# Latent attention: the high and low parts of the values in one stationary, and a left-over column

## The chip, the cores and the metric

One Trainium2 core (trn2) runs the whole encoder layer in one launch. The metric is device microseconds of that core, the median of the runs. A core has five engines with a queue each: TensorE (PE; its weight loads are listed apart as PEld), VectorE (DVE), ScalarE (ACT), GpSimd (POOL) and SyncE (SP), which here only issues DMAs.

## The reference, cut to what matters

The layer has a Fourier mix, a latent attention (MLA), a cross-attention and a mixture of experts. The change is in the latent attention: 8 heads, 2048 queries and keys, 64 + 32 (rotary) dimensions for queries and keys, 64 for values.

```python
kv = (rms_norm(u_kv, g_kv_lat) @ w_kv_up).reshape(B, S, MLA_HEADS, QK_NOPE_DIM + V_HEAD_DIM)
k_nope, v = kv[..., :QK_NOPE_DIM], kv[..., QK_NOPE_DIM:]
...
s = (jnp.einsum("bqhd,bkhd->bhqk", qn_b, k_nope)
     + jnp.einsum("bqhd,bkd->bhqk", qr_b, k_rope))
p = jax.nn.softmax(s.astype(jnp.float32) * scale, axis=-1).astype(v.dtype)
return jnp.einsum("bhqk,bkhd->bqhd", p, v)
```

## The kernel before

All matmuls that matter are done in float32r (R in the code), which keeps fewer bits than float32. So each operand x is held as a high part (x rounded to R) and a low part (x minus the high part, again in R), and a product is three matmuls: high x high, high x low, low x high. `split` makes the two parts, ScalarE the high one by a copy, VectorE the low one by a subtraction; `mm3` does the three matmuls.

**The projection** (`phase_qkv`) makes queries, keys and values in 8 blocks of 256 tokens. `up_v` (L350) projects v for two tiles of 128 tokens, splits it into `vsh` (per head 64 columns and a 65th of ones) and `vsl` (64 columns), and writes both to HBM, `vh_s` and `vl_s`.

**The attention** (`phase_mla`, L850) works in 32 units, head h by chunk c of 512 queries, here named (h,c), and in each over 16 key tiles kt of 128 keys. For a key tile, `scores` (L882) does three matmuls into a PSUM tile `pst` of 128 keys x 512 queries; ScalarE takes the exponential of it twice, once rounded to R (`ph`, L893) and once in full (`pf`, L894); VectorE subtracts to give `pl` (L895). The maximum that keeps the exponential in range was put in as a 97th row of the queries beforehand: `max_steps` (L827) does, during a unit, 16 matmuls into `pmax` and as many VectorE reductions for the next unit, then transposes and copies the result (L845). `values` (L900) does three matmuls into `po`, 65 x 512: values high x ph, low x ph, high x pl. Row 64, from the ones, is the sum of the softmax. After the 16th key tile ScalarE copies `po` out (L911), and two DMAs write it to HBM; the division by the sum comes later, from `os_s`.

**What sets the order.** Nothing is scheduled by a planner; each engine's queue is in the order of the code. Key tile by key tile the loop at L940 does the scores of tile kt, one or two steps of the maximum for the next unit, the values of tile kt-2 (`pend`), and in 92 of 100 tiles one step of a background generator `bg` (`fourier`, L460). In its order, over the stage, the background makes Fourier weights (TensorE, ScalarE, VectorE), squares rows on ScalarE (L544), and four times scales a block x on VectorE (L561: eight products of x with a PSUM tile), folds it on GpSimd (L567 and L568, twice, 128x1024; then eight of 128x512, L583), splits the folds (L36, L37) and multiplies them. Pools set what can run ahead: `pst` has 2 PSUM banks, `po` 2, `pmax` 3, the background 1; `ph` and `pl` have 3 buffers in SBUF, `pf` 2. On GpSimd there is, beside the folds, one memset of a row of ones per head (L816).

The next head's keys and values are loaded by SP during units (h,0) and (h,1).

Of the kernel before, what the change touches and what calls it, by code (L numbers as in the profile page):

```python
# [10 lines left out]
F = mybir.dt.float32  # L11
R = mybir.dt.float32r
# [3 lines left out]
AF = mybir.ActivationFunctionType  # L16
OP = mybir.AluOpType
# [100 lines left out]
def phase_qkv(e):  # L118

    nc, tc = e.nc, e.tc  # L120
    with ExitStack() as ctx:
# [6 lines left out]
        wp = pool(ctx, tc, "wq", side="right")  # L128
# [3 lines left out]
        ps = pool(ctx, tc, "psq", 1, space=PSUM)  # L132
# [37 lines left out]
        vsh = wp.tile([P, H, 2, 65], R, name="vsh")  # L170
        vsl = wp.tile([P, H, 2, 64], R, name="vsl")
        nc.vector.memset(vsh[:, :, :, 64:65].bitcast(F), 1.0)
        xT = e.xT.rearrange("(k p) t -> p k t", p=P)
        XR, XB, SQ, LT, LN, LH = {}, {}, {}, {}, {}, {}

# [174 lines left out]
        def up_v(b):  # L350
            lh, ll = LH[b]
            for t in range(2):
                p = ps.tile([P, 512], F, name="pup", bufs=4)
                tt = slice(t * P, (t + 1) * P)
                for k in range(2):
                    mm3(nc, p, lh[3 + k][:, tt], ll[3 + k][:, tt], wvh[k], wvl[k], k == 0, k == 1)
                split(nc, vsh[:, :, t, 0:64], vsl[:, :, t], p.rearrange("p (h c) -> p h c", h=H))
            eng = nc.scalar if b + 1 == NB else nc.sync
            eng.dma_start(e.vh_s.rearrange("h p c -> p h c")[:, :, 130 * b:130 * b + 130],
                              vsh.rearrange("p h t c -> p h (t c)").bitcast(F))  # L360
            eng.dma_start(e.vl_s.rearrange("h p c -> p h c")[:, :, 128 * b:128 * b + 128],
                              vsl.rearrange("p h t c -> p h (t c)").bitcast(F))
# [12 lines left out]
        for k in range(8):  # L375
            w = wl1(k)
# [16 lines left out]
        for b in range(NB):  # L393
# [34 lines left out]
            elif b + 2 == NB:  # L428
                cs = slice(b * B, (b + 1) * B)
# [420 lines left out]
def phase_mla(e, keep):  # L850

    nc, tc = e.nc, e.tc
    scale = (ND + RD) ** -0.5
    with ExitStack() as ctx:
# [43 lines left out]
        OT = {}  # L898

        def values(h, c, kt, pr):  # L900
            ph, pl = pr
            if kt == 0:
                OT[h, c] = ps.tile([65, 512], F, name="po", bufs=2)
            o = OT[h, c]
            vh, vl = VT[h]
# [3 lines left out]
            if kt == 15:  # L909
                of = mp.tile([65, 512], F, name="of")  # L910
                nc.scalar.activation(of, OT.pop((h, c)), AF.Copy)  # L911
                cs = slice(c * 512, (c + 1) * 512)
                eng = nc.scalar if (h, c) == units[-1] else nc.sync
                eng.dma_start(e.os_s[h:h + 1, cs], of[64:65])
                eng.dma_start(e.o_s[h * 64:(h + 1) * 64, cs], of[0:64])
# [24 lines left out]
        for n, (h, c) in enumerate(units):  # L940
            if n + 3 < len(units):
                load_q(n + 3)
            for kt in range(16):
                if kt in (1, 9) and c < 2 and h + 1 < H:
                    (load_v if c else load_k)(h + 1, kt // 8)
                pend.append((h, c, kt, scores(h, c, kt)))
                for m, i in ahead.get(slot, ()):
                    if i == 0:
                        MX[m] = max_steps(e, QT[units[m]], KT[units[m][0]][0], mp,
                                          lambda shape: ps.tile(shape, F, name="pmax", bufs=3))  # L950
                    MX[m][i]()
                if len(pend) > 2:
                    values(*pend.pop(0))
                slot += 1
                if slot * RATE // 100 > (slot - 1) * RATE // 100:
                    next(bg, None)
                if (h and c == 0 or n == len(units) - 1) and kt in (4, 8, 12):
                    if kt == 4:
                        rs = recip(e, mp, nc.sync, h - 1) if c == 0 else recip(e, mp, nc.sync, h, 0, 1536)
                    next(rs)  # L960
        for u in pend:
            values(*u)
        for _ in bg:
            pass
    e.mx.close()
# [1061 lines left out]
```

## Time and profile before

| | |
|---|---|
| median of 3 runs | 3145.25 us (3144.8 to 3148.56) |
| the profiled execution | 3139.12 us, span 3137.3 us, mean granted clock 0.983 |
| TensorE busy over the span | 3013.9 us, 96% |
| VectorE, ScalarE, GpSimd busy | 1983.7, 1535.0, 485.5 us |
| latent attention | 280.6 to 1264.5 us of the span |

The profile lists instructions by engine, with the line of the kernel, the names of the tiles (out<-in) and their shapes; a line can be a helper's (L36, L37, L44 to L46). "Busy" is time in which an instruction of the engine is listed; matmuls are pipelined, so that one is listed for longer than the distance to the next. What an engine waited for stands in brackets. PEclk is the share of the full TensorE clock that was granted; 1.00 is the upper of its two levels, 2.4 GHz.

### The profile page before, as it was taken

What the parts mean: (1) busy time and instruction counts of PE and PEld (TensorE: products, weight loads), DVE (VectorE), ACT (ScalarE), POOL (GpSimd) and SP (SyncE); (2) the same over time, 40 slices, a digit from 0 to 9 for tenths busy, and PEclk for the clock granted to TensorE, in tenths of its full rate; (3) what the DMA queues carried; (4) which work ended last, traced back from release to release, by engine and by line L of the source; (5) the groups of instructions that cost most, each with busy time, mean ns of one, the idle gap of its engine ahead of it and who ended that gap; (6) DMA issues with size and microseconds to landing.
All of it is one profiled execution on the core that took longest, in us unless ns stands there. A gap on an engine that the chain in (4) does not pass through costs nothing.

```text
span 3137.3 us, 45989 instructions
## 1 busy us (share of the span) xinstructions
PE 3013.9 (96%) x18047; PEld 2560.7 (82%) x18047; DVE 1983.7 (63%) x3481; ACT 1535.0 (49%) x2491; POOL 485.5 (15%) x583
## 2 busy tenths in 40 slices
PE   7999999999999999999999996599999999999998
PEld 6997777677777667789788885599999999999998
DVE  5557878888877776665444445655555555555665
ACT  4444686666666666216433332244444444445554
POOL 1221003221200000101000002100010100003664
PEclk8999999999999999999999998799999999999999
DMA  5766152032121211465111113366767676667885
GB/s 194 216 209 187 47 175 73 22 80 63 28 71 44 71 35 46 145 199 203 57 41 68 55 61 110 130 199 197 221 209 216 212 223 204 209 202 238 302 304 203
DMA packets 322970, 452.46 MB, mean 144 GB/s; under 512 B 21329, under 2 KB 238801, under 8 KB 321410
## 3 DMA queue, kind: packets, MB, share of 16 engines
q1 hardware_dynamic: 290216, 373.08, 37.3%
q0 software_dynamic: 15216, 55.39, 5.8%
q10 hardware_dynamic: 17322, 21.06, 2.2%
q8 instruction: 142, 2.33, 0.3%
q14 instruction: 74, 0.61, 0.1%
HBM read 361.06 MB, written 88.28 MB: 143 GB/s over the span
## 4 chain that ended last, share of the span: by engine, by line
PE 89%; DVE 5%; ACT 2%; issue 2%; DMA 1%; POOL 0%; SPq 0%; POOLq 0%; ACTq 0%; DVEq 0%
PE pa L44 5%; PE pa L45 5%; PE pa L46 5%; PE pb L44 5%; PE pb L45 5%; PE pb L46 5%; PE pst L887 3%; PE pst L889 3%; PE pst L888 3%; PE po L908 3%; PE po L906 3%; PE pmax L835 3%; PE po L907 3%; PE co L44 2%; PE co L46 2%; PE co L45 2%
## 5 line engine op out<-in xcount | busy, mean ns | idle before, releaser
L1671 DVE TENSOR_TENSOR wl<-wr,wh 128x2048 fp32r<-128x2048 f32 x188 | 429.4, 2291 | 263.8 <-ACT wh L1670 263.8
L895 DVE TENSOR_TENSOR pl<-pf,ph 128x512 fp32r<-128x512 f32 x512 | 397.4, 776 | 204.8 <-ACT pf L894 200.2
L893 ACT ACTIVATE ph<-pst 128x512 fp32r<-128x512 f32 x512 | 306.9, 599 | 276.8 <-PE pst L889 273.7
L1670 ACT ACTIVATE wh<-wr 128x2048 fp32r<-128x2048 f32 x191 | 362.8, 1907 | 127.2 <-issue 53.7
L836 DVE TENSOR_REDUCE mt<-pmax 128x1 f32<-128x512 f32 x496 | 337.5, 681 | 0.0
L894 ACT ACTIVATE pf<-pst 128x512 f32<-128x512 f32 x512 | 305.3, 596 | 10.6 <-DVE pl L895 10.5
L44 PE MATMUL pa<-hh,wh 128*128 128x256 f32 x1024 | 292.5, 286 | 0.0
L45 PE MATMUL pa<-hl,wh 128*128 128x256 f32 x1024 | 290.1, 283 | 0.1
L46 PE MATMUL pa<-hh,wl 128*128 128x256 f32 x1024 | 289.8, 283 | 0.0
L45 PE MATMUL pb<-hl,wh 128*128 128x256 f32 x1024 | 289.8, 283 | 0.0
L44 PE MATMUL pb<-hh,wh 128*128 128x256 f32 x1024 | 289.8, 283 | 0.0
L46 PE MATMUL pb<-hh,wl 128*128 128x256 f32 x1024 | 289.7, 283 | 0.0
L908 PE MATMUL po<-pl,vh 128*65 128x512 f32 x512 | 203.0, 396 | 9.2 <-DVE pl L895 9.2
L887 PE MATMUL pst<-q,kl 96*128 96x512 f32 x512 | 206.8, 404 | 1.9 <-ACT pf L894 1.9
L889 PE MATMUL pst<-q,kh 97*128 97x512 f32 x512 | 203.2, 397 | 0.0
L888 PE MATMUL pst<-q,kh 96*128 96x512 f32 x512 | 202.2, 395 | 0.0
L906 PE MATMUL po<-ph,vh 128*65 128x512 f32 x512 | 202.0, 395 | 0.0
L907 PE MATMUL po<-ph,vl 128*64 128x512 f32 x512 | 201.1, 393 | 0.0
L835 PE MATMUL pmax<-kh,q 96*128 96x512 f32 x496 | 198.8, 402 | 1.9 <-DMA q<-qr_s 1.5
L45 PEld LDWEIGHTS pa<-hl,wh 128*128 128x128 f32 x1024 | 196.6, 192 | 1.0 <-DVE hl L37 0.4
L44 PEld LDWEIGHTS pa<-hh,wh 128*128 128x128 f32 x1024 | 196.5, 192 | 0.8 <-ACT hh L36 0.2
L46 PEld LDWEIGHTS pb<-hh,wl 128*128 128x128 f32 x1024 | 196.6, 192 | 0.0
(627 smaller groups left out, 7361.3 us busy)
## 6 DMA issues: line engine op xcount, KB each, us to landing
wr<-in_w_exp_gate SPq DMA_DIRECT2D x64, 1024.0 KB
wr<-in_w_exp_up SPq DMA_DIRECT2D x64, 1024.0 KB
wr<-in_w_exp_down SPq DMA_DIRECT2D x63, 1024.0 KB
xr<-in_xT SPq DMA_DIRECT2D x16, 512.0 KB
wr<-in_x SPq DMA_DIRECT2D x16, 512.0 KB
k_s<-put SPq DMA_DIRECT2D x16, 512.0 KB
q<-q_s SPq DMA_DIRECT2D x32, 256.0 KB
wt<-in_xf SPq DMA_DIRECT2D x32, 256.0 KB
```

The lines of the kernel that those rows point to most:

```text
L44: nc.tensor.matmul(ps, lh, rh, start=start, stop=False, **kw)
L45: nc.tensor.matmul(ps, lh, rl, start=False, stop=False, **kw)
L46: nc.tensor.matmul(ps, ll, rh, start=False, stop=stop, **kw)
L836: nc.vector.tensor_reduce(mt[:, t, j:j + 1], p, axis=AX.X, op=OP.max)
L887: nc.tensor.matmul(p, kl[:, ks], qh[0:96], start=True, stop=False)
L889: nc.tensor.matmul(p, kh[:, ks], qh, start=False, stop=True)
L893: nc.scalar.activation(ph, p, AF.Exp, scale=scale)
L894: nc.scalar.activation(pf, p, AF.Exp, scale=scale)
L895: nc.vector.tensor_sub(pl, pf, ph.bitcast(F))
L908: nc.tensor.matmul(o, vh[:, kt], pl, start=False, stop=kt == 15)
L1670: nc.scalar.activation(W[i][0], r, AF.Copy)
L1671: eng.tensor_sub(W[i][1], r, W[i][0].bitcast(F))
```

## The change

The values of a head are stored as one tile of 129 columns: 64 of the high parts, the ones, the low parts of columns 1 to 63, and as a 129th the low part of column 0. The first 128 are one stationary, and `po` becomes 128 x 512: rows 0 to 63 the high product, row 64 the sum, rows 65 to 127 the low product of columns 1 to 63. `values` does two matmuls with it, against `ph` and against `pl`. The 129th column times `ph` remains, to be added to row 0 of `po`. In six key tiles (`BY_PE`) a matmul with that one column does it. In the other ten, `scores` multiplies `ph` by the column (one number per key, a pointer to 128x1): in six of these on ScalarE, in four on GpSimd (`BY_POOL`); GpSimd adds the ten up in `acc`, and a matmul with ones sums `acc` over the partitions into row 0. This is the new `whole`, which runs before the scores of key tile 3 of the next unit. `whole` also merges the two halves: ScalarE copies rows 64 to 127 into `ol` and once more row 64, the sum, and VectorE adds rows 0 to 63, with `rest` (0 for partition 0, 1 elsewhere) keeping the sum out of row 0.

The second exponential is written over the scores in PSUM (`p`), `pf` goes, and VectorE subtracts from PSUM. `pst` gets 3 banks, `pmax` 2; `ph` 4 buffers, `pl` 2.

```diff
-                split(nc, vsh[:, :, t, 0:64], vsl[:, :, t], p.rearrange("p (h c) -> p h c", h=H))
+                p = p.rearrange("p (h c) -> p h c", h=H)
+                nc.scalar.activation(vs[:, :, t, 0:64], p, AF.Copy)
+                for c, to in ((slice(1, 64), slice(65, 128)), (slice(0, 1), slice(128, 129))):
+                    nc.vector.tensor_sub(vs[:, :, t, to], p[:, :, c], vs[:, :, t, c].bitcast(F))
...
-            p = ps.tile([P, 512], F, name="pst", bufs=2)
+            p = ps.tile([P, 512], F, name="pst", bufs=3)
...
-            ph = pp.tile([P, 512], R, name="ph")
-            pf = pp.tile([P, 512], F, name="pf", bufs=2)
-            pl = pp.tile([P, 512], R, name="pl")
+            ph = pp.tile([P, 512], R, name="ph", bufs=4)
+            pl = pp.tile([P, 512], R, name="pl", bufs=2)
             nc.scalar.activation(ph, p, AF.Exp, scale=scale)
-            nc.scalar.activation(pf, p, AF.Exp, scale=scale)
-            nc.vector.tensor_sub(pl, pf, ph.bitcast(F))
+            nc.scalar.activation(p, p, AF.Exp, scale=scale)
+            nc.vector.tensor_sub(pl, p, ph.bitcast(F))
+
+            if kt not in BY_PE:
+                w = VT[h][:, kt, 128:129].bitcast(F)
+                first = (h, c) not in AC
+                if first:
+                    AC[h, c] = mp.tile([P, 512], R, name="acc", bufs=1)
+                t = AC[h, c] if first else mp.tile([P, 512], F, name="part", bufs=2)
+                if kt in BY_POOL:
+                    nc.gpsimd.tensor_scalar(t, ph.bitcast(F), w, None, op0=OP.mult)
+                else:
+                    nc.scalar.activation(t, ph.bitcast(F), AF.Copy, scale=w)
+                if not first:
+                    nc.gpsimd.tensor_add(AC[h, c], AC[h, c].bitcast(F), t)
...
+        BY_PE, BY_POOL = (0, 1, 2, 7, 12, 15), (4, 6, 9, 11)
...
-            nc.tensor.matmul(o, vh[:, kt], ph, start=kt == 0, stop=False)
-            nc.tensor.matmul(o[0:64], vl[:, kt], ph, start=False, stop=False)
-            nc.tensor.matmul(o, vh[:, kt], pl, start=False, stop=kt == 15)
...
+            for i, t in enumerate(pr):
+                nc.tensor.matmul(OT[h, c], VT[h][:, kt, 0:128], t, start=kt == 0 and i == 0, stop=False, skip_group_check=True)
+            if kt in BY_PE:
+                nc.tensor.matmul(OT[h, c][0:1], VT[h][:, kt, 128:129], pr[0], start=False, stop=False, skip_group_check=True)
+
+        def whole(h, c):
+            o = OT.pop((h, c))
+            nc.tensor.matmul(o[0:1], e.ones[:, 0:1], AC.pop((h, c)), start=False, stop=True, skip_group_check=True)
+            ol = mp.tile([65, 512], F, name="ol", bufs=1)
+            of = ol[0:64]
+            nc.scalar.activation(of, o[64:128], AF.Copy)
+            nc.scalar.activation(ol[64:65], o[64:65], AF.Copy)
+            nc.vector.scalar_tensor_tensor(of, of, rest, o[0:64], op0=OP.mult, op1=OP.add)
...
+                if n and kt == 3:
+                    whole(*units[n - 1])
                 pend.append((h, c, kt, scores(h, c, kt)))
```

How this stands in the queues, first on TensorE before, for one key tile of unit (0,0), from the scores to the values of two tiles earlier:

```order
L887 MATMUL pst_3402<-q_152,kl_150 128x512
L888 MATMUL pst_3402<-q_152,kh_149 128x512
L889 MATMUL pst_3402<-q_152,kh_149 128x512
L835 MATMUL pmax_3412<-kh_149,q_3258 128x512
L906 MATMUL po_3322<-ph_3369,vh_3254 65x512
L907 MATMUL po_3322<-ph_3369,vl_3256 64x512
L908 MATMUL po_3322<-pl_3371,vh_3254 65x512
```

On TensorE with the change, key tile 2 of unit (0,1), the total of unit (0,0) behind it, and the first score of key tile 3:

```order
L887 MATMUL pst_3632<-q_3267,kl_150 128x512
L888 MATMUL pst_3632<-q_3267,kh_149 128x512
L889 MATMUL pst_3632<-q_3267,kh_149 128x512
L837 MATMUL pmax_3641<-kh_149,q_3271 128x512
L924 MATMUL po_3644<-ph_3599,va_3265 128x512
L924 MATMUL po_3644<-pl_3600,va_3265 128x512
L926 MATMUL po_3644<-ph_3599,va_3265 1x512
L930 MATMUL po_3327<-acc_3342,ones_76 1x512
L887 MATMUL pst_3655<-q_3267,kl_150 128x512
```

The three value matmuls have become two, with one of a single column (L926) in six of 16 tiles, and once a unit the matmul of the total (L930).

GpSimd in unit (2,2), before and with the change, where the background's folds d, x and f are made (L567, L568 and L583 have become L569, L570 and L585):

```order
L567 TENSOR_TENSOR d0_6675<-x_6150 128x1024
L568 TENSOR_TENSOR x_6150<-x_6150 128x8x128
L567 TENSOR_TENSOR d1_6710<-x_6150 128x1024
L568 TENSOR_TENSOR x_6150<-x_6150 128x8x128
L583 TENSOR_TENSOR f_6748<-x_6150 128x512
```

```order
L907 TENSOR_TENSOR acc_6645<-acc_6645,part_6733 128x512
L569 TENSOR_TENSOR d0_6741<-x_6210 128x1024
L570 TENSOR_TENSOR x_6210<-x_6210 128x8x128
L903 TENSOR_SCALAR part_6753<-ph_6748,va_4895 128x512
L907 TENSOR_TENSOR acc_6645<-acc_6645,part_6753 128x512
L907 TENSOR_TENSOR acc_6645<-acc_6645,part_6771 128x512
L569 TENSOR_TENSOR d1_6779<-x_6210 128x1024
L570 TENSOR_TENSOR x_6210<-x_6210 128x8x128
L903 TENSOR_SCALAR part_6791<-ph_6786,va_4895 128x512
L907 TENSOR_TENSOR acc_6645<-acc_6645,part_6791 128x512
L585 TENSOR_TENSOR f_6816<-x_6210 128x512
```

Additions of the tiles 8, 9, 10 and 11, and two multiplications, now stand between the folds.

ScalarE with the change, in the same unit, from the exponentials of key tile 13 to those of key tile 15:

```order
L892 ACTIVATE ph_6824<-pst_6820 128x512
L893 ACTIVATE pst_6820<-pst_6820 128x512
L905 ACTIVATE part_6829<-ph_6824,va_4895 128x512
L892 ACTIVATE ph_6841<-pst_6837 128x512
L893 ACTIVATE pst_6837<-pst_6837 128x512
L905 ACTIVATE part_6846<-ph_6841,va_4895 128x512
L847 ACTIVATE q_5853<-pmax_6849 1x512
L37 ACTIVATE fh_6861<-f_6816 128x512
L892 ACTIVATE ph_6869<-pst_6865 128x512
```

Before, only exponentials, L845 (now L847) and the split of f stood there; the scaled copies (L905) of tiles 13 and 14 are new, and each needs one of the two `part` buffers.

## Rows read from the trace of the kernel before

**Rows 1.** Busy time by stretch: the stage, then units (1,0), (1,1), (1,3), (2,2), (3,1), (4,1), (7,3).

```profile
core 0: us, PE busy (x) PEld busy (x) DVE busy (x) ACT busy (x) POOL busy (x), PEclk, DMA share, GB/s
280.60:1264.50 983.90, 966.59 (x4417) 697.89 (x4416) 772.60 (x1224) 660.12 (x1295) 119.77 (x93) 1.00 0.24 66
396.30:424.00 27.70, 26.73 (x117) 18.95 (x116) 20.80 (x34) 25.75 (x64) 1.15 (x1) 1.00 0.90 255
424.00:451.10 27.10, 26.77 (x117) 18.98 (x116) 20.65 (x33) 26.10 (x65) 0.00 (x0) 1.00 0.70 226
478.10:511.40 33.30, 30.49 (x142) 21.67 (x141) 31.47 (x41) 20.18 (x38) 18.93 (x14) 1.00 0.06 16
577.00:608.20 31.20, 27.75 (x118) 18.77 (x118) 30.76 (x42) 19.52 (x36) 14.40 (x6) 1.00 0.07 18
673.10:703.30 30.20, 27.55 (x121) 19.25 (x120) 28.36 (x40) 18.60 (x35) 11.97 (x5) 1.00 0.17 53
...
795.60:829.60 34.00, 31.34 (x147) 22.36 (x146) 30.91 (x42) 20.67 (x40) 14.82 (x8) 1.00 0.17 47
1240.40:1264.50 24.10, 24.04 (x103) 16.35 (x102) 11.90 (x18) 18.33 (x35) 0.00 (x0) 1.00 0.11 29
```

**Rows 2.** Timeline of TensorE over one key tile: start in us, duration in us, instruction.

```profile
703.35 0.39 PE L887 MATMUL pst<-q,kl 96*128 96x512 f32 x1
...
704.27 0.39 PE L906 MATMUL po<-ph,vh 128*65 128x512 f32 x1
704.50 0.40 PE L907 MATMUL po<-ph,vl 128*64 128x512 f32 x1
704.74 0.39 PE L908 MATMUL po<-pl,vh 128*65 128x512 f32 x1
704.97 0.40 PE L887 MATMUL pst<-q,kl 96*128 96x512 f32 x1
```

**Rows 3.** Timeline of ScalarE in unit (1,0), one key tile with a square.

```profile
411.84 0.64 ACT L544 ACTIVATE wt<-wt 128x512 f32<-128x512 f32 x1
412.36 0.21 ACT L544 ACTIVATION_READ_ACCUMULATOR wt<-wt 128x1 f32 x1
412.45 0.61 ACT L893 ACTIVATE ph<-pst 128x512 fp32r<-128x512 f32 x1
412.93 0.62 ACT L894 ACTIVATE pf<-pst 128x512 f32<-128x512 f32 x1
413.41 0.66 ACT L544 ACTIVATE wt<-wt 128x512 f32<-128x512 f32 x1
```

**Rows 4.** Timeline of VectorE and GpSimd in unit (2,2), beside the first folds.

```profile
589.44 0.68 DVE L895 TENSOR_TENSOR pl<-pf,ph 128x512 fp32r<-128x512 f32 x1
589.59 2.79 POOL L567 TENSOR_TENSOR d<-x 128x1024 f32<-128x1024 f32 x1 [55.24 <-DVE x L561]
590.04 0.68 DVE L836 TENSOR_REDUCE mt<-pmax 128x1 f32<-128x512 f32 x1
590.64 0.67 DVE L561 TENSOR_TENSOR x<-x,bg 128x512 f32<-128x512 f32 x1
591.24 1.70 DVE L895 TENSOR_TENSOR pl<-pf,ph 128x512 fp32r<-128x512 f32 x1
```

**Rows 5.** Timeline of ScalarE in the projection: a copy with a pointer as scale, one without.

```profile
55.09 0.71 ACT L39 ACTIVATE wkh<-wr,gk 128x512 fp32r<-128x512 f32 x1
55.70 0.61 ACT L36 ACTIVATE xh<-xr 128x512 fp32r<-128x512 f32 x1
56.23 1.04 ACT L205 ACTIVATE wr<-wr 128x1024 f32<-128x1024 f32 x1
```

**Rows 6.** Groups on VectorE in the stage: count | busy us, mean ns | idle before.

```profile
L895 DVE TENSOR_TENSOR pl<-pf,ph 128x512 fp32r<-128x512 f32 x512 | 397.4, 776 | 204.8 <-ACT pf L894 200.2 <-PE pst L888 1.1 <-PE po L907 0.8
...
L561 DVE TENSOR_TENSOR x<-x,bg 128x512 f32<-128x512 f32 x32 | 21.6, 674 | 0.0
```

**Rows 7.** Groups on GpSimd over the whole span.

```profile
L583 POOL TENSOR_TENSOR f<-x 128x512 f32<-128x512 f32 x16 | 24.7, 1548 | 36.3 <-DVE fl L37 35.9
L567 POOL TENSOR_TENSOR d<-x 128x1024 f32<-128x1024 f32 x8 | 22.3, 2790 | 135.9 <-DVE x L561 135.9
L568 POOL TENSOR_TENSOR x<-x 128x1024 f32<-128x1024 f32 x8 | 21.7, 2718 | 0.6
...
L583 POOL TENSOR_TENSOR f<-d,d 128x512 f32<-128x512 f32 x16 | 20.6, 1287 | 97.9 <-DVE fl L37 97.9
...
L1338 POOL TENSOR_SCALAR h<-x,cy 128x1024 f32<-128x1024 f32 x2 | 2.3, 1128 | 404.4 <-ACT hTh L36 396.9 <-DVE cy L63 7.5
```

**Rows 8.** Busy time in a stretch of the projection, columns as in rows 1.

```profile
150.00:280.00 130.00, 125.21 (x966) 121.06 (x965) 76.37 (x169) 50.81 (x95) 33.30 (x41) 0.97 0.66 204
```

More of the change, by code (lines that the diff above doesn't have):

```diff
@@ L23 @@
 FW, QL, KVL, RD, ND, VD = 512, 384, 256, 32, 64, 64
+VW = 129
 class Env:
@@ L169, in phase_qkv @@
         ssx = wp.tile([P, 16], F, name="ssx")
-        vsh = wp.tile([P, H, 2, 65], R, name="vsh")
-        vsl = wp.tile([P, H, 2, 64], R, name="vsl")
-        nc.vector.memset(vsh[:, :, :, 64:65].bitcast(F), 1.0)
+        vs = wp.tile([P, H, 2, VW], R, name="vs")
+        nc.vector.memset(vs[:, :, :, 64:65].bitcast(F), 1.0)
         xT = e.xT.rearrange("(k p) t -> p k t", p=P)
@@ L356, in up_v @@
                     mm3(nc, p, lh[3 + k][:, tt], ll[3 + k][:, tt], wvh[k], wvl[k], k == 0, k == 1)
-                split(nc, vsh[:, :, t, 0:64], vsl[:, :, t], p.rearrange("p (h c) -> p h c", h=H))
+                p = p.rearrange("p (h c) -> p h c", h=H)
+                nc.scalar.activation(vs[:, :, t, 0:64], p, AF.Copy)
+                for c, to in ((slice(1, 64), slice(65, 128)), (slice(0, 1), slice(128, 129))):
+                    nc.vector.tensor_sub(vs[:, :, t, to], p[:, :, c], vs[:, :, t, c].bitcast(F))
             eng = nc.scalar if b + 1 == NB else nc.sync
[L359 to L362, printed above, removed]
+            eng.dma_start(e.va_s.rearrange("h p c -> p h c")[:, :, 2 * VW * b:2 * VW * (b + 1)],
+                          vs.rearrange("p h t c -> p h (t c)").bitcast(F))
         e.K0 = mla_keys(e, e.m0)
@@ L869, in load_k, with load_v @@
             nc.sync.dma_start(t[64:96].bitcast(F), e.kr_s[:, i])
-        def load_v(h, i, a=0, b=16):
-            n = 65 - i
+        def load_v(h, a, b):
             if a == 0:
-                VT.setdefault(h, []).append(vp.tile([P, 16, n], R, name="vh" if i == 0 else "vl"))
-            t, src = VT[h][i], (e.vh_s, e.vl_s)[i]
-            nc.sync.dma_start(t[:, a:b].rearrange("p t c -> p (t c)").bitcast(F), src[h][:, a * n:b * n])
+                VT[h] = vp.tile([P, 16, VW], R, name="va")
+            nc.sync.dma_start(VT[h][:, a:b].rearrange("p t c -> p (t c)").bitcast(F), e.va_s[h][:, a * VW:b * VW])
         def load_q(n):
@@ L900, in values @@
+            return ph, pl
+        OT, AC = {}, {}
+        BY_PE, BY_POOL = (0, 1, 2, 7, 12, 15), (4, 6, 9, 11)
+        rest = mp.tile([64, 1], F, name="rest", bufs=1)
+        nc.gpsimd.memset(rest, 1.0)
+        nc.gpsimd.memset(rest[0:1], 0.0)
         def values(h, c, kt, pr):
-            ph, pl = pr
             if kt == 0:
-                OT[h, c] = ps.tile([65, 512], F, name="po", bufs=2)
-            o = OT[h, c]
-            vh, vl = VT[h]
-            nc.tensor.matmul(o, vh[:, kt], ph, start=kt == 0, stop=False)
@@ L907, in values @@
-            nc.tensor.matmul(o[0:64], vl[:, kt], ph, start=False, stop=False)
-            nc.tensor.matmul(o, vh[:, kt], pl, start=False, stop=kt == 15)
[L909 to L915, printed above, removed]
+                OT[h, c] = ps.tile([P, 512], F, name="po", bufs=2)
@@ new lines, in values @@
+            for i, t in enumerate(pr):
[10 more added lines that the diff above has]
+            nc.vector.scalar_tensor_tensor(of, of, rest, o[0:64], op0=OP.mult, op1=OP.add)
+            cs = slice(c * 512, (c + 1) * 512)
+            eng = nc.scalar if (h, c) == units[-1] else nc.sync
+            eng.dma_start(e.os_s[h:h + 1, cs], ol[64:65])
+            eng.dma_start(e.o_s[h * 64:(h + 1) * 64, cs], of)
@@ L925, in phase_mla @@
         bg = e.bg
-        for i in range(2):
-            load_v(0, i, 0, 14)
+        load_v(0, 0, 14)
         load_q(1)
         load_q(2)
-        for i in range(2):
-            load_v(0, i, 14, 16)
+        load_v(0, 14, 16)
         ahead, MX = {}, {}
@@ L944, in phase_mla @@
                 if kt in (1, 9) and c < 2 and h + 1 < H:
-                    (load_v if c else load_k)(h + 1, kt // 8)
+                    i = kt // 8
+                    if c:
+                        load_v(h + 1, 8 * i, 8 * i + 8)
+                    else:
+                        load_k(h + 1, i)
+                if n and kt == 3:
+                    whole(*units[n - 1])
                 pend.append((h, c, kt, scores(h, c, kt)))
@@ L949, in phase_mla @@
                         MX[m] = max_steps(e, QT[units[m]], KT[units[m][0]][0], mp,
-                                          lambda shape: ps.tile(shape, F, name="pmax", bufs=3))
+                                          lambda shape: ps.tile(shape, F, name="pmax", bufs=2))
                     MX[m][i]()
@@ L962, in phase_mla @@
             values(*u)
+        whole(*units[-1])
         for _ in bg:
@@ L1873, in run @@
 def run(e):
+    e.va_s = e.tc.dram_tile([H, P, 16 * VW], F, name="va_s")
     with ExitStack() as ctx:
```

1 line of the change is left out of this document (removed).

## The prediction

> **What bounds the kernel now.** I read the windows view first. The change lives in the latent attention, from 280.6 to 1264.5 us, and there TensorE is busy 966.6 of 983.9 us at the full granted clock; VectorE has 772.6, ScalarE 660.1, GpSimd 119.8 [rows 1]. So matmuls taken away count, as far as the engines that get the work can follow. Then the timeline of TensorE, because the durations printed for matmuls overlap: each of the seven matmuls of a key tile is listed with 0.39 to 0.40 us, yet they start 0.23 us apart, seven in 1.62 us [rows 2]. The price of a 512-column matmul is 0.232 us, not 0.395. The width of the stationary makes no difference to it (65 columns in the values, 128 in the scores).
>
> Next, where the stage is not TensorE's. In units (1,0) and (1,1) (396.3 to 451.1 us) ScalarE is busy 25.75 of 27.7 and 26.10 of 27.1 us [rows 1]: the Fourier background squares a row piece in each key tile, and ScalarE runs squares and exponentials without a gap, 1.57 us from one square to the next [rows 3]. And in units (1,3), (2,2), (3,1) and (4,1) TensorE lacks 2.81, 3.45, 2.65 and 2.66 us, 11.6 together [rows 1]: there GpSimd works through its folds, and the subtraction on VectorE with both inputs in SBUF takes 1.70 us beside a fold instead of 0.68, while the product that reads PSUM keeps its 0.67 [rows 4].
>
> **The change part by part.**
>
> *TensorE.* Before, 32 units x 16 tiles x 3 value matmuls = 1536. After, 32 x (16 x 2 + 6 + 1) = 1248. 288 fewer, x 0.232 = **-66.8 us**. The one-column matmul costs a whole 0.232: its 512 moving columns are the same.
>
> *ScalarE.* Added: six scaled copies a unit (192). The nearest row is a copy of 128x512 out of SBUF with a pointer as scale: 0.71 long, the next starts 0.61 later [rows 5]. 192 x 0.61 = 117 us. The output leaves in two copies instead of one, 32 x 0.48 = 15 us. Sum 660 + 132 = 792 of some 940 us: hidden on average, but not in (1,0) and (1,1). There 25.75 + 26.10 + 2 x (6 x 0.61 + 0.48) = 60.1 us, with 0.8 of waits that stay 61.0, where TensorE alone would come to 54.8 - 2 x 9 x 0.232 = 50.6: **+10.4 us** of the gain given back.
>
> *The second exponential in place.* No row shows ScalarE writing PSUM. From PSUM to SBUF it starts every 0.48 us [rows 3]. Below: a copy that reads SBUF takes 0.53 [rows 5], so the side of the memory moves 0.05, and I allow that as a gain, worth under 2 us since ScalarE bounds only two units. Above: reading and writing one bank in turn, twice 0.48. I take 0.48, the row nearest in form. The Trainium skill (ScalarE: Activation LUTs, Step-by-step: what each stage is for) says that ScalarE writes PSUM faster than SBUF, and gives no figure; no run here shows it, and by it the sum would lie toward that lower end.
>
> *VectorE.* The subtraction now reads one input from PSUM. Its mean was 776 ns; the product that also has one input in PSUM takes 674 and is not stretched beside GpSimd [rows 4, 6]. I take 0.67. The 32 new merges of two halves, 64x512, cost at most the same 0.67, 21 us. VectorE loses load on the whole. The Trainium skill (SBUF — State Buffer, Who interferes with whom) has the rule: two SBUF inputs contend with a GpSimd instruction that reads SBUF, one does not. The trace agrees (1.70 against 0.67). By it the subtraction is out of the contention for good; without it, at the stretched length beside a GpSimd that is now busy most of the time, VectorE would be the bound (last rival).
>
> *GpSimd.* Nine additions and four multiplications a unit. Addition 1.29 to 1.55 (a fold of this shape), multiplication half of 1.128 (128x1024) = 0.56 [rows 7]: I take 1.29, since the long value is from folds beside subtractions that will no longer contend. 32 x (11.6 + 2.3) = 443, with the 120 there is 563 of 940 us. The first addend comes at key tile 4, the total is needed before key tile 3 of the next unit, 15 tiles or 22 us later: 13.9 us of work fits, if nothing stands in between.
>
> In four units something does. In (2,2) GpSimd's order after the addition of tile 8 is fold, fold, multiply, add, add, fold, fold, multiply, add: 2 x (2.79 + 2.72) + 2 x 0.56 + 3 x 1.29 = 16.0 us [rows 7]. Tile 8's addition ends about 16 us into the unit (8 tiles x 1.55; 1.8 for 0.7 of scores, 0.48 and 0.6 of exponentials; 0.6; 1.3), so the last of these ends at 32. But "part" has two buffers: ScalarE's scaled copy of tile 14 has to wait for that addition, from 24 to 32, and behind it on ScalarE stand the split of the background's first fold f (ready 1.6 later) and the exponentials of tile 15. Those give TensorE its operand at 36 where it wants it at 27.3 (17.6 tiles x 1.55): 9 us lost. In (3,1) the same count gives f at 35.8, the operand of tile 18 at 38, wanted at 31: 7 us. In (1,3) and (4,1) the folds start between two units, ScalarE is held 2 to 3 us, and TensorE, which can run two tiles ahead, loses about 1.5 each. Together 19, in place of the 11.6 that go with the old contention: **+7.4 us**.
>
> *The rest.* pst gets three banks, pmax two, since PSUM now holds the exponential until the subtraction. pl goes from three to two buffers: the subtraction of tile k waits for the value matmuls of k-2, which stand just behind k's scores and end before k's second exponential does. Nothing. In the last unit ScalarE has 18.3 + 4.1 = 22.5 us where TensorE has 24.1 - 2.1 = 22.0; at the end the total, two copies and the merge stand before the last output DMA, 0 to 3 us; VectorE runs 3 x 0.60 a tile while it scales the background's x, now against tiles of 1.5: some 0.5 each time. **+4 us**. In the projection one more small VectorE instruction a token tile (16 x 0.68 at most, 11 us in 280) lies beside a TensorE that is busy 125.2 of 130 while VectorE has 76.4 [rows 8]; v goes out and comes back in half as many DMAs of the same bytes, so SP's queue only gets shorter. Nothing.
>
> Sum: -66.8 + 10.4 + 7.4 + 4 = **-45 us**. The profiled execution took 3139.1 us for a span of 3137.3, 6 us under the median of 3145.25; the difference goes onto the median: **3100 us**.
>
> **The rivals.**
> 1. *The folds cost little* (GpSimd gets to them later than I count, or the waits overlap): -66.8 + 10.4 - 11.6 + 1 = -67, 3078 us. For it: TensorE's lead, and that each fold's place can slip. Against: GpSimd's order is fixed. 0.14.
> 2. *GpSimd's chain is late in every unit.* At 1.55 to 1.69 an addition and 1.13 a multiplication [rows 7] it is 9 x 1.69 + 4 x 1.13 = 19.7 us plus 3.7 of background, over the 22 us: about 1 us lost a unit, 32 more, 3132 us. It decides from about 2.1 us per addition, or earlier where ScalarE is held by the two parts. 0.13.
> 3. *Slower: the exponential in place takes longer.* ScalarE has 792 us; at 0.96 instead of 0.48 it has 792 + 512 x 0.48 = 1038, and becomes the bound of a stage of 984: +54, 3199 us. From 0.28 us extra per exponential the gain shrinks, from 0.37 it is gone. For it: it reads and writes one bank. Against: nothing, but nothing shows it either. 0.09.
> 4. *The subtraction still collides with GpSimd*: at 1.19 us, halfway from 0.68 to 1.70, VectorE has 772.6 - 397.4 + 512 x 1.19 + 21 = 1006 us [rows 1, 6] and is the bound: +22, 3167 us; it decides from 1.15. Against it stand 32 products at 0.67. 0.03.
>
> **How the numbers follow.** My forecast has 0.60, with 3085 to 3115 as its own range; 0.01 is left for the unforeseen. The range of 3076 to 3126 takes in most of the first rival and the better part of the second, and leaves out the slow cases. A measurement of this kernel tells about 0.2%, 6 us, from no change. Faster: the forecast, the first rival and three quarters of the second, 0.84. Slower: the last two, 0.12. Same: 0.04.
>
> **What would show it.** Right: value matmuls 0.23 apart and 288 fewer; units without background near 25 us; (1,0) and (1,1) longer than before, near 30, with ScalarE without a gap; the subtraction at 0.68 everywhere; waits of ScalarE on GpSimd additions and of TensorE in (2,2) and (3,1). Wrong: exponentials on the same PSUM tile spaced more than 0.55 us; additions over 1.6 us; TensorE waiting for the total at key tile 3 in ordinary units; units (2,2) and (3,1) shorter than 29 us.

## The result, and the profile after

The changed kernel takes 3186.99 us (median of 4 runs, 3185.13 to 3192.9) where the kernel before takes 3146.9: a ratio of 1.0131, interval 1.0113 to 1.0148. It is 40 us slower where 45 us less were forecast, and it lies outside the range.

The windows view of the changed kernel, over the stage and then the units (1,0), (1,1), (1,3), (2,2) and (7,3); columns as in [rows 1]:

```profile
279.50:1307.50 1028.00, 948.47 (x4125) 702.78 (x4123) 765.07 (x1256) 791.66 (x1516) 684.24 (x508) 0.98 0.24 64
402.90:433.70 30.80, 27.92 (x109) 19.83 (x108) 21.50 (x35) 30.66 (x72) 19.56 (x14) 0.94 0.86 240
433.70:464.70 31.00, 27.36 (x108) 18.26 (x107) 21.34 (x34) 30.87 (x73) 17.78 (x13) 1.00 0.62 188
493.90:527.60 33.70, 28.88 (x132) 21.81 (x131) 24.91 (x40) 23.95 (x47) 32.15 (x26) 1.00 0.12 30
596.70:634.20 37.50, 28.75 (x108) 19.73 (x107) 26.71 (x44) 23.35 (x42) 28.27 (x18) 0.85 0.09 25
...
1283.30:1307.70 24.40, 22.35 (x87) 15.30 (x87) 11.94 (x18) 21.25 (x40) 16.99 (x13) 1.00 0.12 28
```

Nearly the whole loss is in the stage: 1028.0 us instead of 983.9, 44 of the 47 us between the two spans (3184.5 and 3137.3). TensorE lacks 17 us of busy time there before [rows 1] and 80 now, so it has become an engine that waits, although no engine has taken its place as the bound: VectorE is busy for 765, ScalarE for 792, GpSimd for 684 us.

The groups of the changed kernel on the engines that took the work (GpSimd's over the span, the others in the stage: count | busy us, mean ns | idle before, and for what):

```profile
L907 POOL TENSOR_TENSOR acc<-acc,part 128x512 fp32r<-128x512 f32 x288 | 377.1, 1309 | 59.4 <-ACT part L905 40.5 <-ACT P4h L37 0.4
L903 POOL TENSOR_SCALAR part<-ph,va 128x512 f32<-128x512 f32 x128 | 205.0, 1601 | 256.9 <-ACT ph L892 142.0 <-PE po L924 74.2 <-PE pst L889 22.9
...
L894 DVE TENSOR_TENSOR pl<-pst,ph 128x512 fp32r<-128x512 f32 x511 | 352.0, 689 | 232.1 <-ACT pst L893 204.9 <-ACT part L905 12.1 <-issue 5.0
...
L893 ACT ACTIVATE pst<-pst 128x512 f32<-128x512 f32 x511 | 303.9, 595 | 0.0
L905 ACT ACTIVATE part<-ph,va 128x512 f32<-128x512 f32 x159 | 113.4, 713 | 23.6 <-POOL acc L907 23.4
```

The exponential in place, the subtraction, the addition and the scaled copy have the forecast prices. ScalarE's sum came out at 792 us, as forecast. The multiplication on GpSimd (L903) has not its price: 1.60 us where 0.56 was forecast.

What TensorE waits for stands in the waits of the changed kernel in the stage (engine, line, released by: us in total, times, longest):

```profile
PEld pmax L837 <- DVE mt L838: 93.9, 138, 2.9
...
PE pmax L837 <- DVE mt L838: 44.7, 63, 2.4
...
PE pmax L837 <- ACT q L847: 15.8, 8, 6.2
PE po L930 <- POOL acc L907: 4.2, 1, 4.2
```

A weight load's wait runs in part beside the matmul ahead of it, so the matmuls' own 44.7 us are nearer to what TensorE lost. Before, the matmul of the maximum waited for hardly anything; in the view of its tile, the waits ahead of `pmax` were these (us, times):

```profile
  DVE mn L839: 7.0, 7
  DVE mt L836: 2.3, 5
```

One such wait, from the timelines of ScalarE, TensorE and VectorE in the changed kernel (start in us, duration, engine, instruction, in brackets the wait), put in order of time, with the rows of other key tiles left out:

```profile
1139.75 0.50 PE L837 MATMUL pmax<-kh,q 96*128 96x512 f32 x1
...
1141.92 0.60 ACT L892 ACTIVATE ph<-pst 128x512 fp32r<-128x512 f32 x1 [0.17 <-POOL acc L907]
1142.41 0.59 ACT L893 ACTIVATE pst<-pst 128x512 f32<-128x512 f32 x1
1142.66 0.40 PE L889 MATMUL pst<-q,kh 97*128 97x512 f32 x1
1143.04 0.69 DVE L894 TENSOR_TENSOR pl<-pst,ph 128x512 fp32r<-128x512 f32 x1 [1.10 <-ACT pst L893]
1143.65 0.68 DVE L838 TENSOR_REDUCE mt<-pmax 128x1 f32<-128x512 f32 x1
1144.38 0.50 PE L837 MATMUL pmax<-kh,q 96*128 96x512 f32 x1 [1.32 <-DVE mt L838]
```

Read it from the end. The last matmul wants the bank that the first one filled, and that the reduction L838 has to empty. The reduction could have started at 1140.3, but on VectorE's queue it stands behind the subtraction of its key tile, and that waits for both exponentials of the tile. ScalarE was late with them here because two copies of the background had waited for VectorE (1.53 and 0.29 us). With three banks TensorE had one more key tile of time before it met this; with two, a ScalarE two tiles late stops it.

### The profile page after: what moved, and what is told of

It reads as the page before. It is cut to its first block, busy times and chain, and to the rows that moved or that the text cites. A ratio compares the mean times of both kernels' runs of the same rounds, so it can differ in the third digit from the quotient of the medians.

```text
span 3184.5 us, 46707 instructions
## 1 busy us (share of the span) xinstructions
PE 3000.1 (94%) x17759; PEld 2568.6 (81%) x17759; DVE 1979.5 (62%) x3529; ACT 1669.3 (52%) x2715; POOL 1049.7 (33%) x1001
## 4 chain that ended last, share of the span: by engine, by line
PE 55%; DVE 3%; issue 1%; POOL 1%; ACT 1%; DMA 0%; POOLq 0%; ACTq 0%; DVEq 0%
PE pa L45 5%; PE pa L46 5%; PE pa L47 5%; PE pb L45 5%; PE pb L46 5%; PE pb L47 5%; PE co L45 2%; PE co L47 2%; PE co L46 2%; PE sc L45 2%; PE sc L47 2%; PE sc L46 2%; PE py L45 2%; PE py L47 2%; PE py L46 2%
## 5 line engine op out<-in xcount | busy, mean ns | idle before, releaser
L894 DVE TENSOR_TENSOR pl<-pst,ph 128x512 fp32r<-128x512 f32 x512 | 352.7, 689 | 234.3 <-ACT pst L893 207.1
L907 POOL TENSOR_TENSOR acc<-acc,part 128x512 fp32r<-128x512 f32 x288 | 377.1, 1309 | 59.4 <-ACT part L905 40.5
L838 DVE TENSOR_REDUCE mt<-pmax 128x1 f32<-128x512 f32 x496 | 337.1, 680 | 0.0
L893 ACT ACTIVATE pst<-pst 128x512 f32<-128x512 f32 x512 | 304.5, 595 | 0.0
L1735 POOL DMA_INDIRECT x_s<-y,idx x24 | 62.9, 2620 | 731.6 <-ACT y L1870 637.6
L903 POOL TENSOR_SCALAR part<-ph,va 128x512 f32<-128x512 f32 x128 | 205.0, 1601 | 256.9 <-ACT ph L892 142.0
L837 PE MATMUL pmax<-kh,q 96*128 96x512 f32 x496 | 213.2, 430 | 63.5 <-DVE mt L838 44.7
L924 PE MATMUL po<-pl,va 128*128 128x512 f32 x512 | 205.7, 402 | 2.7 <-DVE pl L894 2.6
L924 PE MATMUL po<-ph,va 128*128 128x512 f32 x512 | 206.1, 403 | 1.2 <-ACT ph L892 1.2
L837 PEld LDWEIGHTS pmax<-kh,q 96*128 96x128 f32 x496 | 95.3, 192 | 134.3 <-DVE mt L838 93.9
```

The lines of the kernel that those rows point to most:

```text
L837: nc.tensor.matmul(p, qh[0:96, t * P:(t + 1) * P], kh[0:96, j * 512:(j + 1) * 512], start=True, stop=True)
L838: nc.vector.tensor_reduce(mt[:, t, j:j + 1], p, axis=AX.X, op=OP.max)
L893: nc.scalar.activation(p, p, AF.Exp, scale=scale)
L894: nc.vector.tensor_sub(pl, p, ph.bitcast(F))
L907: nc.gpsimd.tensor_add(AC[h, c], AC[h, c].bitcast(F), t)
L924: nc.tensor.matmul(OT[h, c], VT[h][:, kt, 0:128], t, start=kt == 0 and i == 0, stop=False, skip_group_check=True)
```

## The experiments

Each was timed beside runs of the kernel before on the same chip, whose median was between 3143.2 and 3144.6 us; ratios are to that.

**1. The bank alone**, in the kernel before:

```diff
-                                          lambda shape: ps.tile(shape, F, name="pmax", bufs=3))
+                                          lambda shape: ps.tile(shape, F, name="pmax", bufs=2))
```

> The kernel before with one edit: pmax has two PSUM banks instead of three. Theory A (the banks): the maximum matmul of tile k+2 waits for VectorE's reduction of tile k, which stands behind the subtraction of tile k, which waits for both exponentials; so already before any work is shared out, TensorE waits on pmax for 15 to 40 us and the time is 3160 to 3185. Theory B (the load: added copies on ScalarE, and GpSimd multiplications of 1.6 us, hold the units back): no difference beyond 6 us from 3147.

Measured: 3183.37 us, 1.0132 (1.0115 to 1.0149). This one number makes the kernel before as slow as the changed one. Its waits have the same pair (weight load, then matmul):

```profile
PEld pmax L835 <- DVE mt L836: 58.1, 81, 2.4
...
PE pmax L835 <- DVE mt L836: 31.6, 52, 2.2
```

**2. VectorE's reduction ahead of the subtraction**, in the changed kernel; both banks stay two:

```diff
-            nc.vector.tensor_sub(pl, p, ph.bitcast(F))
...
                     MX[m][i]()
+                ph, pl, p = pend[-1][3]
+                nc.vector.tensor_sub(pl, p, ph.bitcast(F))
```

> The changed kernel with one edit: VectorE's reduction of the maximum is issued ahead of the subtraction of the same tile, so that pmax comes free without waiting for the exponentials; same banks, same work on every engine. Theory A: TensorE's waits on pmax for a reduction, 45 us of its own and 94 of its weight loads in the changed kernel, fall below 20, and the time falls by 60 to 100 us, to 3085 to 3125. Theory B: the waits move to other instructions, and the time stays above 3165.

Measured: 3144.67 us, 0.9999 (0.9989 to 1.0009), 42 us under the changed kernel and between the two forecasts. Of the 42, about 9 are in unit (0,0), where the maximum of the next unit makes up to two steps a tile: 38.6 us in the changed kernel, 29.5 here. The matmul's wait for the reduction falls from 44.7 to 13.9 us. So the wait for the bank is about as large as the whole loss, but something else still eats the gain. Its waits in the stage show what is next:

```profile
ACT part L904 <- POOL acc L906: 30.8, 25, 5.9
...
PE pst L889 <- ACT q L847: 15.6, 9, 7.8
PE pmax L837 <- DVE mt L838: 13.9, 18, 1.4
```

**3. The bank given back to the maximum**, at the cost of the scores, order as in the change:

```diff
-            p = ps.tile([P, 512], F, name="pst", bufs=3)
+            p = ps.tile([P, 512], F, name="pst", bufs=2)
...
-                                          lambda shape: ps.tile(shape, F, name="pmax", bufs=2))
+                                          lambda shape: ps.tile(shape, F, name="pmax", bufs=3))
```

> The changed kernel with pmax at three banks and pst at two, as they were before; the exponential stays in place. Theory A: waits on pmax go, but now the scores of tile k+2 wait for the subtraction of tile k, which ends about as late as the reduction did: 3120 to 3175, with the wait now at the first score matmul. Theory B: above 3175, with TensorE waiting for units that ScalarE or GpSimd hold.

Measured: 3172.84 us, 1.0096 (1.0079 to 1.0113). The wait moves to the other tile:

```profile
PEld pst L887 <- DVE pl L894: 116.3, 212, 2.1
...
PE pst L887 <- DVE pl L894: 38.1, 65, 1.7
```

Now that the second exponential stays in PSUM until the subtraction, two banks are too few for the scores as well. Three of each was not tried: it takes one bank more than either kernel uses.

**4. The left-over column on TensorE in all 16 tiles**, nothing on ScalarE or GpSimd, order and banks as in the change:

```diff
-        BY_PE, BY_POOL = (0, 1, 2, 7, 12, 15), (4, 6, 9, 11)
+        BY_PE, BY_POOL = tuple(range(16)), ()
```

> The changed kernel with the left-over column done by TensorE in all 16 tiles: no scaled copies on ScalarE, nothing of it on GpSimd, and no total; TensorE has 1536 value matmuls as before. The banks stay at two for pmax. Theory A: TensorE's waits on pmax stay at 40 us or more over both its queues together, and the time is 3155 to 3190. Theory B: with the load gone the time is that of the kernel before or less, 3130 to 3150.

Measured: 3172.94 us, 1.009 (1.0067 to 1.0113). The kernel is slow without any shared work, 28 us over the kernel before with as many matmuls, so the sharing is not the cause of most of the loss.

**5. GpSimd's multiplication in another form**, in the kernel of experiment 2:

```diff
-                    nc.gpsimd.tensor_scalar(t, ph.bitcast(F), w, None, op0=OP.mult)
+                    nc.gpsimd.tensor_scalar(t, ph.bitcast(F), w, 1.0, op0=OP.mult, op1=OP.mult)
```

> The kernel with the reduction ahead of the subtraction, and GpSimd's four multiplications of a unit written with two operations (times w, times 1.0), the form that the kernel has on 128x1024 elements in 1.128 us. What is asked is the price. Theory C (the rest of the loss is GpSimd's chain: a multiplication of 1.59 us where 0.56 was forecast makes 18 us of GpSimd a unit, so that a scaled copy on ScalarE waits for its buffer, and behind it the 97th row and the exponentials): if the two-op form takes 0.6 us the chain is 14 us and the time falls to 3115 to 3135; if it takes 1.5 us or more, 3140 to 3150. Theory D (ScalarE's own added work, 6 scaled copies of 0.71 us a unit, is the rest of the loss): 3140 to 3150 whatever the form costs.

Measured: 3120.44 us, 0.9914 (0.9897 to 0.993): theory C. GpSimd's groups:

```profile
L906 POOL TENSOR_TENSOR acc<-acc,part 128x512 fp32r<-128x512 f32 x288 | 374.8, 1301 | 132.3 <-ACT part L904 116.8 <-ACT P4h L37 0.8 <-DVE pl L980 0.3
L902 POOL TENSOR_SCALAR part<-ph,va 128x512 f32<-128x512 f32 x128 | 94.3, 736 | 243.4 <-ACT ph L892 118.6 <-PE po L923 86.4 <-PE pst L889 21.4
```

The same product with a second operation that does nothing takes 0.74 us instead of 1.59, and GpSimd now waits 116.8 us for ScalarE's parts, where it waited 33.2 in experiment 2, while ScalarE's wait for GpSimd's additions falls from 30.8 us to 12.6.

**6. The maximum begun earlier**, in the kernel of experiment 2:

```diff
-        LEAD, RATE = 4, 92
+        LEAD, RATE = 8, 92
```

> The kernel with the reduction ahead of the subtraction, and the maximum of the next unit begun 8 key tiles ahead instead of 4, so that ScalarE's copy of the 97th row of the queries stands four tiles earlier. If the late row at the start of a unit is what costs (the waits of the first score matmul for it are 15.6 + 19.9 us in the stage): 3110 to 3130. If the row only shows a ScalarE that is late anyway (theories C and D), the same lateness comes out at the exponentials: 3138 to 3150.

Measured: 3142.69 us, 0.999 (0.9979 to 1.0). The late row of the queries only showed a late ScalarE. Taken away, the wait comes out elsewhere; the weight load of the maximum waits 40.9 us in the stage, up to 8.1 at once.

**7. The four multiplications given to TensorE**, in the kernel of experiment 2:

```diff
-        BY_PE, BY_POOL = (0, 1, 2, 7, 12, 15), (4, 6, 9, 11)
+        BY_PE, BY_POOL = (0, 1, 2, 4, 6, 7, 9, 11, 12, 15), ()
```

> The kernel with the reduction ahead of the subtraction, and the four tiles of a unit that GpSimd multiplied given to TensorE's one-column matmul: 128 matmuls more, 0.232 us each or +29.7 us if TensorE is the bound all along, and GpSimd left with 5 additions of 1.31 us a unit. Theory C: the waits for GpSimd's parts go and give back more than half of that, 3140 to 3160. Theory D: nothing comes back, 3165 to 3180.

Measured: 3120.3 us, 0.9916 (0.9899 to 0.9932), better than either theory had it. 128 matmuls more than in experiment 2, and 24 us less: without the multiplications of 1.59 us more waits went than the matmuls cost. It is also the time of experiment 5: beside these 128 matmuls, the four tiles on GpSimd in the cheap form save nothing, so TensorE's count alone no longer sets the time.

**8. The four multiplications on VectorE**, behind the subtraction, in the kernel of experiment 2:

```diff
+                if LATE:
+                    t, ph, w = LATE.pop()
+                    nc.vector.tensor_scalar(t, ph.bitcast(F), w, None, op0=OP.mult)
+                    nc.gpsimd.tensor_add(AC[h, c], AC[h, c].bitcast(F), t)
```

> The kernel with the reduction ahead of the subtraction, and the four multiplications of a unit on VectorE, behind the subtraction of the same tile, instead of GpSimd: VectorE gets 4 times about 0.65 us a unit (from 128x256 in 0.349 us), GpSimd goes from 18 to 12 us. Theory C: ScalarE's waits for a part go, 3110 to 3135, unless VectorE's folds in seven of the units give part of it back. Theory D: 3140 to 3155.

Measured: 3133.81 us, 0.9957 (0.9941 to 0.9974). Better than on GpSimd at 1.59, worse than at 0.74: VectorE gets 76.8 us more work, and the weight load of the maximum waits 40.4 us for its reductions where it waits 27.4 in experiment 5. That this wait is the whole difference isn't shown.

**9. The two-operation form alone**, the edit of experiment 5 in the changed kernel, the reduction still last:

```diff
-                    nc.gpsimd.tensor_scalar(t, ph.bitcast(F), w, None, op0=OP.mult)
+                    nc.gpsimd.tensor_scalar(t, ph.bitcast(F), w, 1.0, op0=OP.mult, op1=OP.mult)
```

> The changed kernel with GpSimd's multiplication in the form with two operations (0.74 us instead of 1.59), and the reduction still behind the subtraction. The two losses as separate ones: the cheaper form gives back what it gave with the reduction first, 24 us (from 3144.7 to 3120.4), so 3160 to 3166. Rival, one loss inside the other: the bank wait, which every ordinary tile has, hides what the GpSimd chain costs, so the form alone gives under 8 us, 3179 to 3187. Second rival, the bank wait comes from exponentials that GpSimd's chain makes late: over 40 us come back, below 3147.

Measured: 3170.12 us, 1.0074 (1.0055 to 1.0094), 17 us under the changed kernel. That is between the theory and its first rival. With the reduction first the form gave 24; the intervals are too wide to tell 17 from 24, so the two losses are about separate, and at most overlap a little. The wait for the bank does not come from GpSimd's multiplication: the weight load's wait for the reduction stays at 93.7 us (140 times) beside 93.9.

**10. The share set by unit**, in the kernel of experiment 5:

```diff
+        NO_POOL, NO_ACT = ((2, 2), (2, 3), (3, 2), (4, 0), (6, 1)), ((1, 0), (1, 1))
+        def on_pe(h, c, kt):
+            if kt in BY_PE:
+                return True
+            return (h, c) in (NO_POOL if kt in BY_POOL else NO_ACT)
```

> The kernel with the reduction first and the two-op form, and the share set by unit: in (1,0) and (1,1), where ScalarE's squares make 30 to 31 us, ScalarE's six tiles go to TensorE (six one-column matmuls of 0.232 us, 1.4 us a unit); in (2,2), (2,3), (3,2), (4,0) and (6,1), where GpSimd has bursts, GpSimd's four go to TensorE (0.93 us a unit). Units as the runs so far had them: the burst units come out as with no GpSimd multiplication (11 us less in sum), the two others at 28 to 29 us instead of 30 to 31 (4 us less): 3100 to 3110. If the lateness only moves on to the next unit, 3115 to 3122.

Measured: 3113.94 us, 0.9906 (0.989 to 0.9923), the fastest of all, though its interval overlaps that of experiment 5. Windows of (1,0), (1,1), (2,2) and (2,3):

```profile
387.00:415.50 28.50, 27.25 (x114) 18.93 (x113) 21.36 (x35) 26.11 (x63) 8.78 (x9) 1.00 0.88 232
415.50:443.50 28.00, 27.03 (x114) 19.17 (x113) 21.20 (x34) 27.81 (x67) 6.66 (x7) 1.00 0.76 235
563.60:589.80 26.20, 26.20 (x113) 18.94 (x112) 24.32 (x41) 21.70 (x40) 12.38 (x7) 1.00 0.08 21
589.80:626.40 36.60, 33.56 (x161) 26.59 (x160) 27.03 (x42) 25.84 (x50) 18.17 (x15) 0.95 0.06 15
```

The first two came as expected. Of the units with folds, (2,2) and (2,3) together fell only from 66.9 us in experiment 5 to 62.8. Where one ends and the other begins depends on the matmul from which one counts: these windows start at the third score matmul, and that one waits 6.87 us for the 97th row at the start of (2,3) in experiment 5. Counted so, (2,2) fell from 32.8 to 26.2 and (2,3) rose from 34.1 to 36.6; from the first score matmul, (2,2) stays at 26 and (2,3) falls from 41.1 to 36.6. Either way (2,3) is still longer than the 32.6 us of the kernel before, though GpSimd has only the folds and the additions there.

**11. The reduction first, in the kernel before**, with its three banks:

```diff
-            nc.vector.tensor_sub(pl, pf, ph.bitcast(F))
...
+                ph, pl, pf = pend[-1][3]
+                nc.vector.tensor_sub(pl, pf, ph.bitcast(F))
```

> The kernel before with the one change that VectorE's reduction stands ahead of the subtraction of the same tile, and three banks for the maximum as it has them. Theory: with three banks the maximum waited 9.3 us in the whole stage, so the order is worth little by itself: 3138 to 3146, and the gain of the later versions comes from fewer matmuls. Rival: the order is a gain of its own, with or without the change: 3120 to 3135.

Measured: 3144.98 us, 1.0005 (0.9995 to 1.0015). The order is worth nothing where the bank doesn't wait.

**12. Experiments 2 and 4 together**: all on TensorE, reduction first.

```diff
-        BY_PE, BY_POOL = (0, 1, 2, 7, 12, 15), (4, 6, 9, 11)
+        BY_PE, BY_POOL = tuple(range(16)), ()
...
-            nc.vector.tensor_sub(pl, p, ph.bitcast(F))
...
+                nc.vector.tensor_sub(pl, p, ph.bitcast(F))
```

> The kernel with the left-over column on TensorE in all 16 tiles of a unit (as many value matmuls as before the change, no scaled copy, no GpSimd share) and the reduction ahead of the subtraction. It tells what the sharing itself is worth once neither the bank nor GpSimd holds it. Theory: TensorE is the bound where nothing is late, so this is 288 matmuls of 0.232 us (66.8 us) over the sharing kernels less what ScalarE's and GpSimd's lateness costs them (20 to 30 us): 3140 to 3165, by TensorE's count nearest to 3146, that of before. Rival: the one-column form costs TensorE more than the 64-column one it replaces: over 3165. Second rival, TensorE is not the bound and the sharing is worth nothing: 3115 to 3130.

Measured: 3128.91 us, 0.9954 (0.9939 to 0.9969). That was under every case but the last, and not for that one's reason, since TensorE is busy for 964 of 971 us. This kernel has as many matmuls as the one before, and yet is faster. The units that are shorter are those with folds: (1,3), (2,2), (3,1) and (4,1) have 29.6, 26.7, 27.3 and 30.4 us where they had 33.3, 31.2, 30.2 and 34.0 [rows 1], 14.7 together. The subtraction's group on VectorE in (1,3), first of the kernel before:

```profile
L895 DVE TENSOR_TENSOR pl<-pf,ph 128x512 fp32r<-128x512 f32 x18 | 19.9, 1106 | 1.4 <-ACT pf L894 1.4
```

and of this one:

```profile
L979 DVE TENSOR_TENSOR pl<-pst,ph 128x512 fp32r<-128x512 f32 x17 | 11.6, 684 | 2.1 <-ACT pst L893 2.0
```

Beside GpSimd's folds the subtraction took 1.11 us and now takes 0.68. The order is not the cause: experiment 11 has it too, with both inputs in SBUF, and takes 1.17 in the same stretch, while experiment 4, with one input in PSUM and the old order, takes 0.69. It is the input from PSUM.

## Why the prediction was wrong, point by point

**TensorE's count and price: right.** The page lists 17759 matmuls instead of 18047, 288 fewer, and the one-column matmul takes its 0.23 us like any other (1141.96 to 1142.19, in the changed kernel):

```profile
1141.72 0.40 PE L924 MATMUL po<-pl,va 128*128 128x512 f32 x1
1141.96 0.40 PE L926 MATMUL po<-ph,va 128*1 128x512 f32 x1
1142.19 0.40 PE L887 MATMUL pst<-q,kl 96*128 96x512 f32 x1
```

**The exponential in place: right**, third rival out. It takes 595 ns, and in the timeline above the next instruction starts 0.52 us after it, where 0.48 was forecast. The Trainium skill (ScalarE: Activation LUTs, Step-by-step: what each stage is for) says that ScalarE writes PSUM faster than SBUF. No run here shows it: the first exponential, which writes SBUF, takes 595 ns too, and the second one of the kernel before, which also wrote SBUF, was followed after 0.48 us [rows 3]. By these rows the write to PSUM is no gain.

**The subtraction: right**, fourth rival out: 689 ns against 776 [rows 6], and beside folds 684 against 1106 (experiment 12). By the rule of the Trainium skill (SBUF — State Buffer, Who interferes with whom) on two SBUF inputs it should come out so, and the traces agree. The folds d and x on GpSimd also fell, from 2.79 and 2.72 [rows 7] to 2.4 us.

**Units (1,0) and (1,1): right.** 61.8 us together where 61.0 was forecast, ScalarE without a gap; experiment 10 takes the copies away and gets 56.5.

**The folds in (2,2): the mechanism right, the size near**, first rival out. The scaled copy waits for GpSimd's addition, and behind it stand the 97th row, the split of f and the next exponential:

```profile
629.24 1.26 POOL L907 TENSOR_TENSOR acc<-acc,part 128x512 fp32r<-128x512 f32 x1
630.53 0.72 ACT L905 ACTIVATE part<-ph,va 128x512 f32<-128x512 f32 x1 [5.95 <-POOL acc L907]
631.28 0.59 ACT L847 ACTIVATE q<-pmax 1x512 fp32r<-1x512 f32 x1
631.89 0.63 ACT L37 ACTIVATE fh<-f 128x512 fp32r<-128x512 f32 x1
631.92 0.80 PE L837 MATMUL pmax<-kh,q 96*128 96x512 f32 x1 [6.22 <-ACT q L847]
632.52 0.63 PE L924 MATMUL po<-ph,va 128*128 128x512 f32 x1
632.94 0.63 PE L924 MATMUL po<-pl,va 128*128 128x512 f32 x1
```

That unit takes 37.5 us. TensorE's count alone would be 27.75 - 9 x 0.232 = 25.7 [rows 1], so 12 are lost where 9 were forecast; part of that is the clock, which was halved at the end of the unit (last section), and 2.0 us a wait for the maximum's bank. What TensorE waits for at the end of that chain is the bank of the maximum, not the operand of tile 15.

(3,1) itself takes 28.0 us, under the 29 that the prediction named as a sign against it. But its folds are felt behind its end, as the count with tile 18 had it: in the next unit, (3,2), which takes 37.6 us where it took 32.0, ScalarE waits for the fold, and TensorE the 4.2 us for the total that stand among the waits above:

```profile
ACT fh L37 <- POOL f L585: 5.1, 1, 5.1
```

**"pst gets three banks, pmax two ... Nothing": wrong, and the step that failed.** The bank taken from the maximum is worth 39 us (experiment 1) to 42 (experiment 2). The prediction names it and puts it at nothing without a reason: the "Nothing" is argued for `pl` alone. Who empties the bank, and what stands ahead of that instruction on its queue, does not occur in it. None of the rivals had it.

**The multiplication: mis-sized.** 0.56 was half of a 1.13 us row with another form of the instruction, two operations instead of one [rows 7]. It measured 1.60 (and 0.74 in the form of that row, so half was too little even there), and GpSimd's chain 9 x 1.31 + 4 x 1.60 = 18.2 us a unit instead of 13.9. That is near the second rival, which had a chance of 0.13 and came to 19.7 another way, by additions of 1.69 and multiplications of 1.13. Experiments 2 and 5 put it at 24 us, experiment 9 with the changed kernel's last reduction at 17.

**"Hidden on average" of ScalarE's new work: too kind.** The forecast was 87 us below the result. The bank is 42 of them and the multiplication 24; about 20 remain, from 3120 to the forecast of 3100. In the units (4,3), (5,1) to (6,2) and (7,0), where ScalarE has 21 to 28 us of work in about 32, experiment 5 takes 254.6 us, and experiment 12, with 9 matmuls more a unit, 250.6. So there the sharing brought nothing where 9 x 0.232 = 2.1 us a unit were counted. Which wait holds those eight units wasn't settled, and with it the cause of these 20 us stays open: the largest wait on TensorE in that stretch is still the maximum's bank (9.1 us).

All in all, with the reduction first and the cheap form, the sharing itself is worth 8 us (experiment 12 to 5) to 15 (to 10), and the exponential kept in PSUM, with the bank paid for by the order, about as much (experiment 11 to 12, 16 us; the two differ in the layout of the values and the buffers as well).

## What to carry to other kernels

When a tile loses a buffer, look up the instruction that frees it, what stands ahead of it in its engine's queue, and how late that may come; an instruction whose data is ready long before belongs ahead of one that waits. Price an instruction from a row of the same form, engine, size and operand count, not from one that does the same arithmetic. And when a change bundles an edit that saves with one that takes a buffer, time the second alone in the old kernel first: here that was one number.

## What the runs showed of the hardware

**A form of an instruction.** On GpSimd a 128x512 product with a pointer takes 1.59 us with one operation and 0.74 with two (experiment 5). On VectorE the one-operation form has a median of 0.48 us, but 27 of the 128 took over 0.6, and the longest, 3.48 us, lies beside a row of GpSimd's memsets, which only write (experiment 8):

```profile
1067.83 0.96 POOL L731 MEMSET wy<- 72x1024 f32 x1
1068.08 3.48 DVE L983 TENSOR_SCALAR part<-ph,va 128x512 f32<-128x512 f32 x1
...
1070.64 0.63 POOL L743 MEMSET bd<- 128x128 f32 x4
1071.48 0.67 DVE L838 TENSOR_REDUCE mt<-pmax 128x1 f32<-128x512 f32 x1
```

It ends 0.3 us after GpSimd's row of memsets. That GpSimd held it up is read from this overlap; no run takes the memsets away.

**A wait costs the clock as well.** In unit (2,2) of the changed kernel TensorE waits, 2.0 us and then 6.2, and the granted clock falls from 1.00 to 0.50, 1.2 GHz (columns as in [rows 1]):

```profile
615.00:620.00 5.00, 5.00 (x22) 3.83 (x22) 4.35 (x8) 3.25 (x7) 4.92 (x3) 1.00 0.00 0
620.00:625.00 5.00, 2.98 (x11) 2.12 (x11) 1.68 (x3) 2.78 (x5) 4.84 (x4) 0.81 0.00 0
625.00:630.00 5.00, 0.70 (x2) 0.00 (x0) 0.90 (x2) 0.00 (x0) 4.84 (x4) 0.50 0.28 80
630.00:634.20 4.20, 2.28 (x5) 1.83 (x6) 1.51 (x2) 3.03 (x5) 4.20 (x4) 0.50 0.00 0
```

The matmuls behind the wait start 0.42 us apart (632.52 to 632.94 above) instead of 0.23. Over the stage the granted clock is 0.98 where it was 1.00 [rows 1].
